# The second half of the tokens reads x by features, without transposes on TensorE

## The chip, the cores and the metric

The kernel runs on one core of a Trainium2 chip. The metric is the device time of one execution in microseconds, as the median of several runs. The engines are TensorE (PE for its matmuls, PEld for its weight loads), VectorE (DVE), ScalarE (ACT), GpSimd (POOL) and SyncE (SP), which issues most DMAs. Each works through a queue of its own in order; a semaphore wait at its head stops all that is behind it.

## The reference, cut to what matters

One residual block over 1024 tokens of 1024 features, all float32. The first lines are those of the change:

```python
def rms_norm(x, w):
    return x * rsqrt(mean(x * x, axis=-1) + 1e-6) * w

h = rms_norm(x, norm1_w) * (1 + scale1) + shift1      # shift1 .. gate2 from silu(c) @ w_ada + b_ada
x = x + gate1 * (concat[A(h), B(h)] @ w_out)          # A: gated delta rule, 4 heads x 128; B: short convolution
h = rms_norm(x, norm2_w) * (1 + scale2) + shift2
x = x + gate2 * ((silu(h @ w_gate) * (h @ w_up)) @ w_down)
return rms_norm(x, norm_f_w)
```
A and B begin with one projection `h @ w_in`. A's q, k and v go through a causal convolution over four tokens and SiLU, and then through the delta rule, which walks over the tokens in chunks of 64, so that its second half follows its first.

## The kernel before

**The projection.** Features lie on the partitions. `H[k][hf]` holds block k (128 of 1024 features) of h for one half of the tokens (`hf`, 512 tokens), as a high part, rounded for the fast matmul, and a low part, the rest; each product is three 128x512 matmuls (high by high, high by low, low by high). One column tile (128 columns of w_in by one half) is 24 of them into one PSUM bank, `acc` in the trace. `loader` fetches a tile's weights in two units (`raw`), `split_unit` splits each into high (ACT or DVE) and low (DVE), `u` in the trace, and `fill` multiplies. A task such as `q20` names tiles that need the first half alone, `z12` both halves.

**The first half.** x by tokens is normalised and transposed block by block (`xh0`), while the weights of six column tiles come in by DMA (`load0`) and `acc0` multiplies (`acc` from `whl`). Their evacuation is `first_evac`: a copy from PSUM into one of two buffers `pr`, four taps of the convolution on DVE (`cv`), SiLU on ACT.

**The second half.** `h1_load` fetches the four x tiles of tokens 512 to 1023 when the loads of the first half are issued. `norm_rs` squares and sums a tile on ACT (`jk`), adds EPS and takes the power -1/2 on POOL (`st`, `rs`). DVE scales the tile, in place. Then for each feature block `h1_work` transposes four 128x128 pieces on TensorE into a bank (`tr`), and `h_make` evacuates it: high part on ACT, the whole again as `hf` on ACT or DVE, low part on DVE (`h <- hf,h`). Two tasks `h1_work` share the eight blocks.

**What follows.** When all eight blocks stand, `ab_phase(1)` multiplies h by the columns of a and b (`ab`, 16 matmuls), the pool of the x tiles closes and the delta rule `gdn` of the first half may begin (`gT`, `gbc`, `kT`, ... and the chain of `K`, `A`, `O` with the state S), with the column tiles of the projection between its matmuls.

**What sets the order.** Up to the `o` tiles nothing of this order is written by hand. Each part is a task that asks for its next operation; a planner inside the kernel (`Sim`) holds a cost for each operation and emits, engine by engine, the one that can begin first. Within a small tolerance the smaller priority number goes first: `PR` gives `evac` 1.5, `h1` 1.8, `split` 3, `fill` 9. So one number can move every engine's queue. Buffers that the planner hands out it knows; the x tiles (`xp`, eight buffers) are handed out by the pool, and a load into a used buffer gets a semaphore wait of which the planner has no count. The MLP behind the `o` tiles is in an order written by hand.

Of the kernel before, what the change touches and what calls it, by code (L numbers as in the profile page):

```python
# [9 lines left out]
F32 = mybir.dt.float32  # L10
F32R = mybir.dt.float32r
BF16 = mybir.dt.bfloat16
AF = mybir.ActivationFunctionType
ALU = mybir.AluOpType
# [3 lines left out]
P = 128  # L18
# [3 lines left out]
KB = 8  # L22
NT = 8
HT = 512
# [13 lines left out]
HOLD = dict(pe=0.0, dve=0.12, act=0.12, sp=0.0, pool=0.0)  # L38
MARGIN = dict(pe=0.6)
BIAS = dict(dve=0.3)  # L40
PR = dict(sums0=0.35, x0=0.1, ada0=0.2, h0=0.3, w0=0.4, acc=0.5, load0=0.0, setup=0.2, hurry=0.5, chain=0, m=1, evac=1.5, a=2, v=2.5, ab=1.2, out=4, h1=1.8, split=3, y0=5, wu=5.5, x2=6, ada=7, fill=9)
TASKS = "z00 q20 s00 q30 z12 z32 z22 s32 q01 q11 z01 q21 q31 s22 s10 s11 s01".split()
CHUNKS = [(0, 4), (4, 4), (8, 3)]
STEPS = (("X", "A11", "B11", True), ("Y", "A12", "B21", True), ("X", "S2", "T2", False), ("Z", "S1", "T1", True),
# [7 lines left out]
def kernel(  # L52
    ctx: ExitStack,
    tc: tile.TileContext,
    x: bass.AP,
    c_cols: bass.AP,
    cols: bass.AP,
    w_ada: bass.AP,
# [16 lines left out]
    chain, mover = [None], [None]  # L75

    class Ordered:
# [18 lines left out]
    PE, DVE, ACT, POOL, SP = (Ordered(n, e) for n, e in (  # L96
        ("pe", nc.tensor), ("dve", nc.vector), ("act", nc.scalar), ("pool", nc.gpsimd), ("sp", nc.sync)))
# [7 lines left out]
    def nm(s):  # L105
        n_id[0] += 1
        return f"{s}_{n_id[0]}"
# [23 lines left out]
    def flat(ap):  # L131
        return ap.rearrange("p a b -> p (a b)")
# [13 lines left out]
    ident = cst.tile([P, P], F32, name="ident", tag="ident")  # L146
    make_identity(nc, ident)
    ones_r = cst.tile([P, P], F32R, name="ones", tag="ones")
    ones = ones_r.bitcast(F32)
# [11 lines left out]
    def rsqrt_pow(dst, src, n):  # L161
        return POOL.tensor_tensor(dst, src, nhalf[:, 0:n], ALU.pow)
# [7 lines left out]
    def raw_t(shape=(P, HT), dtype=F32):  # L170
        return cyclic("raw", RAW, shape, dtype)
# [10 lines left out]
    sp = s_ctx.__enter__()  # L182
    x_ctx = tc.tile_pool(name="xp", bufs=1, side="left", reuse_waits="tile")
    xp = x_ctx.__enter__()
# [3 lines left out]
    def dma(out, in_):  # L188
        SP.dma_start(out=out, in_=in_)
# [5 lines left out]
    def load_x(tt, pool, tag, bufs):  # L195
        t = pool.tile([P, D], F32, name=nm("x"), tag=tag, bufs=bufs)
        dma(t, xs[tt * P:(tt + 1) * P, :])
        return t
# [3 lines left out]
    def h_slot(k, hf):  # L202
        return hp_.tile([P, 2, HT], F32R, name=nm(f"h{k}_{hf}"), tag=f"H{k}_{hf}")
# [23 lines left out]
    x0 = [xp.tile([P, D], F32, name=nm("x"), tag="x", bufs=8) for _ in range(4)]  # L227
# [13 lines left out]
    for i in range(2):  # L241
        dg = raw_t([P, 4, P])
# [6 lines left out]
    s1c = cst.tile([P, KB], F32, name="s1c", tag="s1c")  # L249
    b1c = cst.tile([P, KB], F32, name="b1c", tag="b1c")  # L250
    nb1 = sp.tile([P, KB], F32, name="nb1", tag="nb1")
    mods = sp.tile([P, 2 * KB], F32, name="mods", tag="mods")

    def norm_rs(t, pool, tag, jt="junk"):
        junk = pool.tile([P, D], BF16, name=nm("jk"), tag=jt, bufs=1)
        st = pool.tile([P, 2], F32, name=nm("st"), tag=tag, bufs=4)
        sq = ACT.activation(junk, t, AF.Square, scale=1.0 / 32.0, accum_out=st[:, 0:1])
        p0 = POOL.tensor_scalar(st[:, 1:2], st[:, 0:1], EPS, None, ALU.add)
        rs = pool.tile([P, 1], F32, name=nm("rs"), tag=tag + "r", bufs=4)
        p1 = rsqrt_pow(rs, st[:, 1:2], 1)  # L260
        return rs, sq, p0, p1

    def xnorm(t, pool):
        rs = norm_rs(t, pool, "n1")[0]
        DVE.tensor_scalar(t, t, rs, None, ALU.mult)

    heads01 = [m0 + hd for hd in (0, 1) for m0 in (MT_K, MT_Q, MT_V)]
    late = []
    for i, t in enumerate(x0):
        rs, sq, p0, p1 = norm_rs(t, sp, "n1")  # L270
# [33 lines left out]
    class Sim:  # L304
# [18 lines left out]
        def free(self, t):  # L323
            res, i = self.owner.pop(t.tensor.name)
            res.slots.append((max([a[4] for a in self.acc.get(t.tensor.name, [])] + [0.0]), i))
            res.slots.sort()
# [228 lines left out]
    hfs, was, wrs, whls = sim.res("hf", 2), sim.res("wa", 5), sim.res("wr", 3), sim.res("whl", 2)  # L555
    raws, hls = sim.res("raw", RAW), sim.res("hl", 4)
    prs, cvs, vts, qks = sim.res("pr", 2), sim.res("cv", 2), sim.res("vT", 4), sim.res("qkT", 4)
    dense, chb = sim.res("b", 3), sim.res("b", 5, (6, 7, 3, 4, 5))
# [6 lines left out]
    def bank(res, name):  # L565
        return res.tile(psp, [P, HT], F32, name)
# [7 lines left out]
    free = sim.free  # L574
# [12 lines left out]
    def mm(out_, lhsT, rhs, start=True, stop=True):  # L587
        PE.matmul(out_, lhsT, rhs, start=start, stop=stop)

    def tr(out_, in_):  # L590
        PE.transpose(out_, in_, ident)
# [49 lines left out]
    def h_make(k, h, ps, first=None):  # L641
        hf = hfs.tile(sp, [P, HT], F32, "hf")
        ACT.activation(h[:, 0, :], ps, AF.Identity, bias=b1c[:, k:k + 1], scale=s1c[:, k:k + 1])
        if first is not None:
            first[k] = h
        if first and k:
            ACT.activation(hf, ps, AF.Identity, bias=b1c[:, k:k + 1], scale=s1c[:, k:k + 1])
        else:
            sim.either([("act", "activation", nc.scalar.activation, (hf, ps, AF.Identity), dict(bias=b1c[:, k:k + 1], scale=s1c[:, k:k + 1])),
                        ("dve", "tensor_scalar", nc.vector.tensor_scalar, (hf, ps, s1c[:, k:k + 1], b1c[:, k:k + 1], ALU.mult, ALU.add), {})])  # L650
        free(ps)
        DVE.tensor_tensor(h[:, 1, :], hf, h[:, 0, :].bitcast(F32), ALU.subtract)
        free(hf)
# [140 lines left out]
        free(scr)  # L794
        sc_[hf] = dict(beta=beta, G=G, nG=nG, eG=eG, kd=kd)

    x1 = []

    def h1_load():
        sim.wait(lambda: "loads0" in done)  # L800
        for tt in range(4, 8):
            x1.append(load_x(tt, xp, "x", 8))
        for t in x1:
            xnorm(t, sp)
        done.add("x1")

    h1_left = list(range(KB))
# [1 line left out]
    def h1_work():  # L809
        sim.wait(lambda: "x1" in done)  # L810
        while h1_left:
            k = h1_left.pop(0)
            ps = bank(chb, "tr")
            for i in range(4):
                tr(ps[:, i * P:(i + 1) * P], x1[i][:, k * P:(k + 1) * P])
            h = h_slot(k, 1)
            h_make(k, h, ps)
            H[k][1] = h
            if all(H[j][1] is not None for j in range(KB)):
                done.add("h1")  # L820
# [76 lines left out]
    def loader():  # L897
        sim.wait(lambda: "loads0" in done)
        while todo:
            sim.wait(lambda: any(may(kd_, hv_) for kd_, _, hv_ in todo))  # L900
            kind, i, halves = todo.pop(next(n for n, (kd_, _, hv_) in enumerate(todo) if may(kd_, hv_)))
            for c0, hs, evac, start in tiles_of(kind, i, halves):
# [4 lines left out]
                for n in range(2):  # L907
# [3 lines left out]
                    dma(flat(r), w_in[(c0 if c0 < AB_COL else c0 - 8) // P, :, n * HT:(n + 1) * HT])  # L911
                    sim.spawn(split_unit, lambda: PR["hurry"] if ready_u[0] < 2 else PR["split"], it, n, r)
        done.add("loaded")
# [10 lines left out]
    def fill():  # L924
        while True:
# [4 lines left out]
            for hf in it["halves"]:  # L930
                ps = bank(dense, "acc")
                for k in range(KB):
# [270 lines left out]
    def gdn(hf):  # L1203
# [252 lines left out]
    x2 = []  # L1456
# [10 lines left out]
    for _ in range(2):  # L1467
        sim.spawn(h1_work, PR["h1"])
# [253 lines left out]
    c = {p: {} for p in range(NP)}  # L1722
# [316 lines left out]
    def prod_d(ci, s, i):  # L2039
        b, an, bn, first = STEPSD[s]  # L2040
        nf = CHUNKS[ci][1]
        sets = ((2, 3, 6, 7), (4, 5, 0, 1))
        if first:
            bd_[b, i] = bank_tile(sets[(ci + (b != "X")) % 2][i], "dn")
        ps = bd_[b, i]
        sl = slice(i * P, (i + 1) * P)
        for j in range(nf):
            a, u = dm[ci, an][j], dm[ci, bn][j]
            for m, (ai, ui) in enumerate(((0, 0), (0, 1), (1, 0))):
                pmm(ps, a[ai][:, sl], u[ui], first and j == 0 and m == 0, j == nf - 1 and m == 2, not first)  # L2050
        return ps
# [55 lines left out]
    for k, (n, i) in enumerate(slots):  # L2107
        ci, s = seq_d[n]
        ps = prod_d(ci, s, i)
# [24 lines left out]
def _laid_out(a):  # L2134
    import numpy as np

    col = lambda v: v.reshape(-1, P).T
    w, wi = a["w_ada"][0], a["w_in"][0]
    d = {n: a[n] for n in ("x", "w_ada", "b_ada", "A_log", "dt_bias", "w_out", "w_gate", "w_up", "w_down", "norm_f_w")}
    d["c_cols"] = col(a["c"])  # L2140
    d["cols"] = np.concatenate([col(a[n]) for n in ("norm1_w", "b_ada", "norm2_w", "gdn_norm_w", "conv_qkv_w", "conv_short_w")], axis=1)
    d["w_mod"] = w[:, 0:2 * D].T.reshape(2, KB, P, D).transpose(1, 2, 0, 3)
    d["w_in0"] = wi[:, 0:1536].reshape(KB, P, 3, 512)[:, :, :, 0:256].reshape(KB, P, 768)
    main = np.concatenate([wi[:, 0:AB_COL], wi[:, SCB_COL:]], axis=1)
    d["w_in"] = main.reshape(KB, P, -1, P).transpose(2, 1, 0, 3).reshape(-1, P, D)
    d["w_ab"] = wi[:, AB_COL:SCB_COL].reshape(KB, P, 8).transpose(1, 0, 2).reshape(P, 64)
    d["consts"] = _constants()
    return d


_ARGS = ["x", "c_cols", "cols", "w_ada", "w_mod", "b_ada", "w_in0", "w_in", "w_ab", "A_log", "dt_bias", "w_out",
         "w_gate", "w_up", "w_down", "norm_f_w", "consts"]


# [34 lines left out]
```

## Time and profile before

| | |
|---|---|
| median of 3 runs | 1169.83 us (1169.58 to 1169.99) |
| profiled execution | 1169.63 us, of which the span of the trace is 1167.8 us |
| busy: PE, PEld, DVE, ACT, POOL | 1157.2, 968.1, 920.7, 546.1, 59.6 us |
| DMA | 207.06 MB, 177 GB/s on the mean |
| granted TensorE clock | 0.999 |

In the profile "line engine operation out<-in" names a group of instructions by the tiles that it writes and reads, without their numbers; `L450` and `L88` are helpers through which all instructions pass, so tiles and not lines tell them apart. Before, `L450` is the planned part and `L88`, `L89` the parts in a fixed order. A row of a timeline has the start, the length of a merged group and its count; a float32 matmul on plain float32 counts as two records, a transpose as one. In a list of waits the columns are total, times and longest. An order (below) lists what stands in an engine's queue, not when it runs.

### The profile page before, as it was taken

The page shows a single profiled execution, that of the slowest core. Times are in us where ns is not written, and L with a number is a line of the kernel's source. Part 1 is how long each engine was busy: PE and PEld are TensorE (multiplying, and loading weights), DVE is VectorE, ACT ScalarE, POOL GpSimd, SP SyncE. Part 2 cuts the span into 40 slices and gives each one's busy share as a digit, 9 for nine tenths or more (in the row PEclk, how much of TensorE's full clock was granted, in tenths as well). Part 3 has the DMA queues.
Part 4 walks back from the last instruction along what each step waited for, and adds up shares of the span by engine and source line. Part 5 has one row for each costly group of instructions (what it writes and reads, how often), then busy time and mean ns, then how long its engine had stood idle before and what let it go on. Part 6 is the DMA issues. An engine that isn't in the chain of part 4 may idle for free.

```text
span 1167.8 us, 16456 instructions
## 1 busy us (share of the span) xinstructions
PE 1157.2 (99%) x5582; PEld 968.1 (83%) x5582; DVE 920.7 (79%) x1702; ACT 546.1 (47%) x1182; POOL 59.6 (5%) x100
## 2 busy tenths in 40 slices
PE   9999999999999999999999999999999999999997
PEld 7888888888888888888888888888888888888886
DVE  7898988898987898669776777776777687788676
ACT  6779733458634552325433333333333365443343
POOL 1110101001101010200000000000000000000002
PEclk9999999999999999999999999999999999999999
DMA  9633455534325555434264456446554589869413
GB/s 363 246 99 110 118 171 163 168 114 137 113 66 163 163 193 175 174 101 144 80 216 158 140 201 223 159 132 222 191 184 137 194 306 393 308 203 340 144 37 145
DMA packets 126453, 207.06 MB, mean 177 GB/s; under 512 B 20513, under 2 KB 45089, under 8 KB 126369
## 3 DMA queue, kind: packets, MB, share of 16 engines
q1 hardware_dynamic: 121520, 202.86, 51.5%
q10 hardware_dynamic: 4848, 3.15, 0.9%
q8 instruction: 44, 0.72, 0.3%
q14 instruction: 41, 0.33, 0.1%
HBM read 150.91 MB, written 55.05 MB: 176 GB/s over the span
## 4 chain that ended last, share of the span: by engine, by line
PE 93%; DVE 3%; ACT 2%; DMA 1%; issue 1%; SPq 0%; ACTq 0%; DVEq 0%
PE acc L88 35%; PE acc L450 24%; PE dn L88 17%; PE o L88 4%; PE o L450 4%; PE A L450 1%; PE K L450 1%; DMA wr<-in_w_in_dram 1%; DVE xo L89 1%; PE ab L450 1%; PE w L450 1%; PE u L450 1%; PE O L450 1%; PE tr L450 1%; PE kk L450 1%
## 5 line engine op out<-in xcount | busy, mean ns | idle before, releaser
L450 PE MATMUL acc<-h,u 128*128 128x512 f32 x1200 | 301.0, 398 | 0.0
L450 PEld LDWEIGHTS acc<-h,u 128*128 128x128 f32 x1200 | 219.0, 188 | 41.1
L88 PE MATMUL acc<-h,hl 128*128 128x512 f32 x600 | 140.1, 390 | 0.0
L88 PEld LDWEIGHTS acc<-h,hl 128*128 128x128 f32 x600 | 112.4, 188 | 23.2
L88 PE MATMUL acc<-h,u 128*128 128x512 f32 x456 | 106.1, 389 | 0.0
L88 PE MATMUL acc<-T,hl 128*128 128x512 f32 x432 | 101.4, 390 | 0.4 <-ACT cc L89 0.4
L88 PEld LDWEIGHTS acc<-h,u 128*128 128x128 f32 x456 | 85.6, 188 | 17.7
L88 PEld LDWEIGHTS acc<-T,hl 128*128 128x128 f32 x432 | 80.9, 188 | 17.5 <-ACT cc L89 0.9
L88 PE MATMUL dn<-h,h 128*128 128x512 f32 x396 | 90.7, 389 | 0.0
L89 DVE TENSOR_TENSOR xo<-xo,dn 128x512 f32<-128x512 f32 x84 | 57.0, 683 | 42.3 <-PE dn L88 34.8
L89 ACT COPY cc<-acc 128x512 f32<-128x512 f32 x66 | 38.4, 590 | 108.3 <-PE acc L88 108.3
L88 PEld LDWEIGHTS dn<-h,h 128*128 128x128 f32 x396 | 74.3, 188 | 15.4
L88 PE MATMUL acc<-T,u 128*128 128x512 f32 x360 | 84.0, 389 | 0.0
L88 PEld LDWEIGHTS acc<-T,u 128*128 128x128 f32 x360 | 67.6, 188 | 14.0
L450 ACT CAST u<-raw 128x512 fp32r<-128x512 f32 x69 | 42.7, 622 | 66.0 <-PE acc L450 64.3
L89 DVE TENSOR_TENSOR cc<-cc,acc 128x512 f32<-128x512 f32 x66 | 43.8, 682 | 29.8 <-PE acc L88 29.8
L89 DVE TENSOR_TENSOR hl<-R,hl 128x512 fp32r<-128x512 f32 x60 | 39.4, 687 | 33.5 <-ACT hl L89 33.4
L450 DVE TENSOR_TENSOR u<-raw,u 128x512 fp32r<-128x512 f32 x82 | 56.0, 685 | 11.9 <-ACT u L450 11.7
L450 DVE SCALAR_TENSOR_TENSOR cv<-pr,cols_a,cv 128x512 f32<-128x512 f32 x72 | 52.9, 745 | 0.1
L89 ACT CAST h<-rw 128x512 fp32r<-128x512 f32 x57 | 32.7, 618 | 40.5 <-PE dn L88 34.6
L89 ACT CAST hl<-R 128x512 fp32r<-128x512 f32 x60 | 35.7, 622 | 23.5 <-DVE R L89 10.7
L89 DVE TENSOR_TENSOR u<-R,u 128x512 fp32r<-128x512 f32 x46 | 30.1, 686 | 20.6 <-ACT u L89 20.5
(343 smaller groups left out, 1993.2 us busy)
## 6 DMA issues: line engine op xcount, KB each, us to landing
raw<-in_w_in_dram SPq DMA_DIRECT2D x82, 256.0 KB, 3.1
am_scr<-cc SPq DMA_DIRECT2D x77, 256.0 KB, 4.6
raw<-in_w_ada_dram SPq DMA_DIRECT2D x56, 256.0 KB, 3.4
rw<-am_scr SPq DMA_DIRECT2D x55, 256.0 KB, 5.2
rw<-bm_scr SPq DMA_DIRECT2D x53, 256.0 KB, 5.3
bm_scr<-raw SPq DMA_DIRECT2D x51, 256.0 KB, 5.4
R<-in_w_gate_dram SPq DMA_DIRECT2D x22, 512.0 KB, 4.3
R<-in_w_up_dram SPq DMA_DIRECT2D x22, 512.0 KB, 5.5
```

Of the source, the lines that this page charges most:

```text
L88: return call(*a, **k)
L89: ins = call(*a, **k)
L450: ins = call(*a, **k)
```

## The change

The host lays out a second copy of the second half's x, by features (`x_t`, eight blocks of 128 features by 512 tokens). `h1_load` fetches four tiles of two blocks each (`xt`). The x by tokens is still fetched and squared, for the norm alone: `norm_rs` writes the four factors into the columns of `rs1`; a diagonal of them is multiplied by ones on TensorE, one plain float32 matmul 128x512, which puts the factor of token c into column c of all partitions (`RS`). For each block DVE makes `hf` = xt * scale column * RS, ACT adds the bias into the high part, and DVE makes the low part from `hf`, bias and high part. The scaling of x on DVE, the 32 transposes and the evacuations of their banks go. `h1` gets priority 1.3 instead of 1.8, ahead of `evac`.

```diff
-PR = dict(... evac=1.5, a=2, v=2.5, ab=1.2, out=4, h1=1.8, split=3, ...)
+PR = dict(... evac=1.5, a=2, v=2.5, ab=1.2, out=4, h1=1.3, split=3, ...)
...
-    def norm_rs(t, pool, tag, jt="junk"):
+    def norm_rs(t, pool, tag, jt="junk", rs=None):
...
-        rs = pool.tile([P, 1], F32, name=nm("rs"), tag=tag + "r", bufs=4)
+        if rs is None:
+            rs = pool.tile([P, 1], F32, name=nm("rs"), tag=tag + "r", bufs=4)
...
-    x1 = []
+    x1t, rs1 = [], sp.tile([P, 4], F32, name="rs1", tag="rs1")
+    RS = sp.tile([P, HT], F32, name="RS", tag="RS")
 
     def h1_load():
         sim.wait(lambda: "loads0" in done)
-        for tt in range(4, 8):
-            x1.append(load_x(tt, xp, "x", 8))
-        for t in x1:
-            xnorm(t, sp)
+        for j in range(4):
+            t = xp.tile([P, 2, HT], F32, name=nm("xt"), tag="x", bufs=8)
+            dma(t, x_t[2 * j:2 * j + 2].rearrange("k p c -> p k c"))
+            x1t.append(t)
+        for i in range(4):
+            t = load_x(4 + i, xp, "x", 8)
+            norm_rs(t, sp, "n1", rs=rs1[:, i:i + 1])
+        dg = raw((P, 4, P))
+        DVE.tensor_tensor(dg, bc1(ident, 4), bc2(rs1, P), ALU.mult)
+        ps = bank(chb, "RS")
+        mm(ps, ones, flat(dg))
+        free(dg)
+        ecopy(RS, ps)
+        free(ps)
         done.add("x1")
...
             k = h1_left.pop(0)
-            ps = bank(chb, "tr")
-            for i in range(4):
-                tr(ps[:, i * P:(i + 1) * P], x1[i][:, k * P:(k + 1) * P])
             h = h_slot(k, 1)
-            h_make(k, h, ps)
+            hf = hfs.tile(sp, [P, HT], F32, "hf")
+            DVE.scalar_tensor_tensor(hf, x1t[k // 2][:, k % 2], s1c[:, k:k + 1], RS, ALU.mult, ALU.mult)
+            ACT.activation(h[:, 0, :], hf, AF.Identity, bias=b1c[:, k:k + 1])
+            DVE.scalar_tensor_tensor(h[:, 1, :], hf, b1c[:, k:k + 1], h[:, 0, :].bitcast(F32), ALU.add, ALU.subtract)
+            free(hf)
             H[k][1] = h
...
+    d["x_t"] = a["x"][0, HT:].T.reshape(KB, P, HT)
```

Three places of the new order. TensorE first, in the column tiles after `ab` of the first half. Before, transposes of a block stand between the matmuls of a tile:

```order
L450 MATMUL acc_771<-h_0_86_518,u_695 128x512 x2
L450 MATMUL tr_821<-ident,x_405 128x128
L450 MATMUL tr_821<-ident,x_428 128x128
L450 MATMUL tr_821<-ident,x_436 128x128
L450 MATMUL tr_821<-ident,x_441 128x128
L450 MATMUL acc_771<-h_0_86_518,u_695 128x512
```
The change has one row in their place, 26 matmuls behind `ab` of the first half:

```order
L448 MATMUL acc_559<-h_0_86_519,u_464 128x512 x3
L448 MATMUL acc_707<-h_0_37_240,u_565 128x512 x2
L448 MATMUL RS_698<-raw_677,ones 128x512
L448 MATMUL acc_707<-h_0_37_240,u_565 128x512
L448 MATMUL acc_707<-h_0_44_274,u_565 128x512 x3
```
After RS 70 matmuls follow (the rest of three tiles), and then the 16 of `ab` of the second half, the last two of them on the last block; before, these stand behind the last transposes, later by 35 matmuls. From the products `P` of the second half's delta rule on, both orders are the same on TensorE.

DVE, at the end of the work on the second half's h. Before, the low parts stand singly among taps of the convolution (`cv`) and low parts of weights (`u`):

```order
L450 TENSOR_TENSOR h_1_135_757<-hf_758,h_1_135_757 128x512
L450 TENSOR_TENSOR u_795<-raw_773,u_795 128x512
L450 SCALAR_TENSOR_TENSOR cv_814<-pr_790,cols_a,cv_814 128x512
L450 MEMSET pr_831 128x3
L450 SCALAR_TENSOR_TENSOR cv_814<-pr_790,cols_a,cv_814 128x512
L450 COPY halo<-pr_831 128x3
L450 TENSOR_SCALAR cv_852<-pr_831,cols_a 128x512
L450 SCALAR_TENSOR_TENSOR cv_814<-pr_790,cols_a,cv_814 128x512
L450 TENSOR_TENSOR u_829<-raw_801,u_829 128x512
L450 SCALAR_TENSOR_TENSOR cv_852<-pr_831,cols_a,cv_852 128x512
L450 TENSOR_TENSOR h_1_148_826<-hf_827,h_1_148_826 128x512
```
In the change (`hf` from `xt`, then the low part of h) the taps of the two first-half tiles `cv_730` and `cv_757` are left until the last blocks are done:

```order
L448 TENSOR_TENSOR u_823<-raw_804,u_823 128x512
L448 TENSOR_SCALAR raw_694<-raw_694 128x16
L448 SCALAR_TENSOR_TENSOR hf_842<-xt_443,s1c,RS 128x512
L448 SCALAR_TENSOR_TENSOR h_1_155_835<-hf_836,b1c,h_1_155_835 128x512
L448 SCALAR_TENSOR_TENSOR cv_730<-pr_689,cols_a,cv_730 128x512
L448 SCALAR_TENSOR_TENSOR h_1_157_841<-hf_842,b1c,h_1_157_841 128x512
L448 SCALAR_TENSOR_TENSOR cv_730<-pr_689,cols_a,cv_730 128x512
L448 SCALAR_TENSOR_TENSOR cv_757<-pr_732,cols_a,cv_757 128x512
L448 TENSOR_TENSOR u_850<-raw_828,u_850 128x512
L448 SCALAR_TENSOR_TENSOR cv_757<-pr_732,cols_a,cv_757 128x512
```
Their buffers `pr` come free only behind them, and the next column tiles are copied out of PSUM into those buffers.

SP's queue, behind the small loads of `setup`. Before, four x tiles and then the weights of the first column tiles:

```order
L450 DMA raw_420<-in_w_ab_dram 128x64
L450 DMA x_405<-in_x_dram 128x1024
L450 DMA x_428<-in_x_dram 128x1024
L450 DMA x_436<-in_x_dram 128x1024
L450 DMA x_441<-in_x_dram 128x1024
L450 DMA raw_406<-in_w_in_dram 128x512
L450 DMA raw_452<-in_w_in_dram 128x512
```
In the change the tiles by features come first, and the x by tokens, the first of which goes into a buffer of the first half's x, stand among the weights:

```order
L448 DMA raw_422<-in_w_ab_dram 128x64
L448 DMA xt_407<-in_x_t_dram 128x2x512
L448 DMA xt_430<-in_x_t_dram 128x2x512
L448 DMA xt_438<-in_x_t_dram 128x2x512
L448 DMA xt_443<-in_x_t_dram 128x2x512
L448 DMA x_448<-in_x_dram 128x1024
L448 DMA raw_408<-in_w_in_dram 128x512
L448 DMA raw_459<-in_w_in_dram 128x512
L448 DMA raw_563<-in_w_in_dram 128x512
L448 DMA x_575<-in_x_dram 128x1024
```

More of the change, by code (lines that the diff above doesn't have):

```diff
@@ L40 @@
 BIAS = dict(dve=0.3)
-PR = dict(sums0=0.35, x0=0.1, ada0=0.2, h0=0.3, w0=0.4, acc=0.5, load0=0.0, setup=0.2, hurry=0.5, chain=0, m=1, evac=1.5, a=2, v=2.5, ab=1.2, out=4, h1=1.8, split=3, y0=5, wu=5.5, x2=6, ada=7, fill=9)
+PR = dict(sums0=0.35, x0=0.1, ada0=0.2, h0=0.3, w0=0.4, acc=0.5, load0=0.0, setup=0.2, hurry=0.5, chain=0, m=1, evac=1.5, a=2, v=2.5, ab=1.2, out=4, h1=1.3, split=3, y0=5, wu=5.5, x2=6, ada=7, fill=9)
 TASKS = "z00 q20 s00 q30 z12 z32 z22 s32 q01 q11 z01 q21 q31 s22 s10 s11 s01".split()
@@ L55 @@
     x: bass.AP,
+    x_t: bass.AP,
     c_cols: bass.AP,
@@ L258, in norm_rs @@
         p0 = POOL.tensor_scalar(st[:, 1:2], st[:, 0:1], EPS, None, ALU.add)
-        rs = pool.tile([P, 1], F32, name=nm("rs"), tag=tag + "r", bufs=4)
+        if rs is None:
+            rs = pool.tile([P, 1], F32, name=nm("rs"), tag=tag + "r", bufs=4)
         p1 = rsqrt_pow(rs, st[:, 1:2], 1)
         return rs, sq, p0, p1
-    def xnorm(t, pool):
-        rs = norm_rs(t, pool, "n1")[0]
-        DVE.tensor_scalar(t, t, rs, None, ALU.mult)
     heads01 = [m0 + hd for hd in (0, 1) for m0 in (MT_K, MT_Q, MT_V)]
@@ L2148, in _laid_out @@
     return d
-_ARGS = ["x", "c_cols", "cols", "w_ada", "w_mod", "b_ada", "w_in0", "w_in", "w_ab", "A_log", "dt_bias", "w_out",
+_ARGS = ["x", "x_t", "c_cols", "cols", "w_ada", "w_mod", "b_ada", "w_in0", "w_in", "w_ab", "A_log", "dt_bias", "w_out",
          "w_gate", "w_up", "w_down", "norm_f_w", "consts"]
```

## The prediction

> **What bounds the kernel now.** I read the page first, then TensorE's waits, its busy time by stretch, and the timeline of the stretch that the change touches.
>
> ```profile
> span 1167.8 us, 16456 instructions
> PE 1157.2 (99%) x5582; PEld 968.1 (83%) x5582; DVE 920.7 (79%) x1702; ACT 546.1 (47%) x1182; POOL 59.6 (5%) x100
> PE 93%; DVE 3%; ACT 2%; DMA 1%; issue 1%; SPq 0%; ACTq 0%; DVEq 0%
> ```
> The last line is the chain that ended last by engine. 93% of it is TensorE. The waits of TensorE's matmuls over the whole span (in total, times, longest), and three stretches (length, busy time of PE, PEld, DVE, ACT, POOL, then clock, DMA share, GB/s), say the same:
>
> ```profile
> PE heat L88 <- POOL nhalf L89: 1.4, 1, 1.4
> PE acc L450 <- ACT h L450: 1.1, 1, 1.1
> PE acc L88 <- ACT cc L89: 0.4, 1, 0.4
> PE y L450 <- DVE pr L450: 0.4, 1, 0.4
> PE A L450 <- DVE S L450: 0.2, 1, 0.2
> PE ps L88 <- DVE raw L89: 0.2, 1, 0.2
> ```
>
> ```profile
> 16.00:52.00 36.00, 36.00 (x170) 29.26 (x169) 31.74 (x59) 26.42 (x47) 2.37 (x5) 1.00 0.90 348
> 52.00:90.00 38.00, 38.00 (x187) 31.43 (x186) 36.25 (x76) 28.88 (x49) 5.37 (x6) 1.00 0.25 80
> 1150.00:1168.00 18.00, 11.12 (x49) 8.85 (x48) 11.08 (x19) 7.00 (x18) 3.73 (x7) 0.93 0.47 174
> ```
> All waits come to 3.7 us, and 6.9 lie behind the last matmul (18.00 - 11.12); with the busy 1157.2 that is the whole span. So an instruction taken out of its queue is worth what it holds there, as long as nothing new makes it wait. The second stretch is that of the change: DVE is busy 36.25 of 38 us in it, and that is where a new wait could come from.
>
> A busy share alone would not prove this. The Trainium skill says so (Perfetto Trace Analysis, Identifying the Most-Contended Engine): matmul occupancy is a poor measure for TensorE, and weight loads tell more. Here those are at 83%, so by that page alone the transposes might lie in slack, and the sum would be near zero. What decides is the start-to-start spacing below.
>
> **Transposes removed.** A stretch of TensorE's timeline (start, length of the merged group, instruction, count):
>
> ```profile
> 66.57 6.64 PE L450 MATMUL acc<-h,u 128*128 128x512 f32 x28
> 73.05 0.60 PE L450 MATMUL tr<-ident,x 128*128 128x128 f32 x4
> 73.40 4.83 PE L450 MATMUL acc<-h,u 128*128 128x512 f32 x20
> ...
> 85.72 1.18 PE L450 MATMUL acc<-h,u 128*128 128x512 f32 x4
> 86.74 0.60 PE L450 MATMUL tr<-ident,x 128*128 128x128 f32 x4
> ```
> From a group of four transposes to the next matmul are 73.40 - 73.05 = 0.35 us. Eight such groups are 2.8 us. There is a second cost, at the edges. 28 matmuls take 73.05 - 66.57 = 6.48 us, 4 take 86.74 - 85.72 = 1.02: 24 more cost 5.46, or 0.2275 each, so the run of four pays 0.11 beyond 4 x 0.2275. Each interruption of the 128x512 stream costs about that; eight go, 0.9 us. Together -3.7 us.
>
> The duration column reads otherwise:
>
> ```profile
> L450 PE MATMUL tr<-ident,x x64: 270/272/273, 8.8 to 87.1; 128*128 128x128 f32 x64
> ```
> 272 ns is what one transpose shows, though the starts are 0.09 us apart. The Trainium skill (TensorE: Matmul & The Clock Gate, Part 4: PE-mode transpose) gives about 275 ns for one inside a kernel. The trace agrees on that as a latency. Taken as a price, 32 of them are 8.8 us instead of 3.7, and the time would be about 1161.5 us (an estimate from that page). The spacing of starts decides against it.
>
> **One matmul added: RS.** It is 128x512 on plain float32, a kind that runs before only at the very start (two in the first two rows below). Its warm neighbour is a group of four 128x128 float32 products, also 512 columns:
>
> ```profile
> 3.70 2.61 PE L88 MATMUL ps<-raw,ones 128*128 128x512 f32 x4 [0.18 <-DVE raw L89]
> 6.14 2.84 PE L88 MATMUL heat<-ident,ones 128*128 128x128 f32 x24
> ...
> 109.49 1.05 PE L450 MATMUL kk<-qkT 128*128 128x128 f32 x8
> 110.30 0.48 PE L450 MATMUL acc<-h,u 128*128 128x512 f32 x1
> ```
> Ends: 0.81 us (110.30 - 109.49) and 1.22 us ((6.14 - 3.70) / 2, waits included). I take 0.81, the warm one, plus one interruption: +0.9 us.
>
> **Order on TensorE elsewhere.** The other matmuls are the same ones, planned into another order up to about 260 us. Counted in the two orders, the 128x512 stream is broken 11 times less often; eight minus one are explained above, four are chance merges of small groups: -0.4 us. Sum on TensorE: -3.7 + 0.9 - 0.4 = -3.2 us.
>
> **DVE and ACT.** Prices and places, single rows out of the timelines of DVE, ACT, POOL and PE (STT is the scalar_tensor_tensor):
>
> ```profile
> 50.50 0.75 DVE L450 TENSOR_SCALAR x<-x,rs 128x1024 f32<-128x1024 f32 x1
> 51.16 4.06 DVE L450 SCALAR_TENSOR_TENSOR cv<-pr,cols_a,cv 128x512 f32<-128x512 f32 x6
> 67.56 0.81 DVE L450 TENSOR_SCALAR hf<-tr,s1c,b1c 128x512 f32<-128x512 f32 x1 [0.28 <-ACT h L450]
> 89.34 0.69 DVE L450 TENSOR_TENSOR h<-hf,h 128x512 fp32r<-128x512 f32 x1 [0.38 <-ACT hf L450]
> 86.00 0.78 ACT L450 ACTIVATE h<-tr,b1c,s1c 128x512 fp32r<-128x512 f32 x1
> 47.10 1.65 ACT L450 CAST u<-raw 128x512 fp32r<-128x512 f32 x3
> 55.75 0.59 ACT L450 COPY raw<-ab 128x512 f32<-128x512 f32 x1 [0.49 <-PE ab L450]
> 57.90 1.04 ACT L450 ACTIVATE jk<-x 128x1024 bf16<-128x1024 f32 x1
> 59.84 1.02 POOL L450 TENSOR_TENSOR rs<-st,nhalf 128x1 f32<-128x1 f32 x1
> 51.88 3.83 PE L450 MATMUL ab<-h,wab 128*128 128x512 f32 x16
> 55.55 2.21 PE L450 MATMUL acc<-h,u 128*128 128x512 f32 x9
> ```
> DVE loses four scalings of x (3.0 us), one hf (0.8) and eight subtractions (5.5), and gains 16 STT at 4.06 / 6 = 0.68 (10.8) and the diagonal for RS (0.7): +2.2 us net. ACT drops 15 passes over PSUM at 0.78 and gains eight from SBUF (0.55, as the casts) and one copy (0.59): about -6.7 us. Neither sets the end by itself, so I cost both at nothing, if TensorE stays covered. The cover: RS stands 26 matmuls and a group of transposes after 55.55, at about 62.0 us, and ends at 62.9; its copy on ACT (0.6) lets DVE begin at 63.5. From there to the last h DVE has 18 STT (16 for h, two of the conv), five lo parts of weights at 0.69 and small ones: 12.2 + 3.6, so the last h stands at about 79.3 us (in before, 89.34 + 0.69 = 90.0). TensorE reaches `ab` of this half 70 matmuls after RS, at 78.9 us, but needs the last h only with the last of its 16, at 82.4. Margin 3 us. One wait is new: RS waits for the diagonal, that for the fourth x's norm on POOL, and every matmul behind RS stands with it. In the new order the fourth square follows ACT's copy of `ab` directly, at 56.3; from a square's begin to POOL's end are 59.84 + 1.02 - 57.90 = 3.0 us, the diagonal takes 0.7, so RS could run from about 60.0 and stands at 62.0. Margin 2 us.
>
> **DMA.** 2 MB more are read, and the new x tiles lie in the buffers of the first half's x, whose last transposes run at 40.44:
>
> ```profile
> 35.27 3.91 SPq L450 DMA_DIRECT2D x<-in_x_dram x4
> 39.76 20.27 SPq L450 DMA_DIRECT2D raw<-in_w_in_dram x8
> ...
> 40.44 0.60 PE L450 MATMUL tr<-ident,x 128*128 128x128 f32 x4
> ```
> SP's queue stands at the first x until about 41.0, so the w_in loads behind it issue some 2 us later, with 0.5 MB (1.5 us at 348 GB/s) ahead of them. They are cast from 47.1 on and multiplied from 55.55 on: 3.5 us late at most, hidden by some 5 us. If the cover were gone, they would cost those 3.5.
>
> **Waits that stay.** The first chain of the delta rule and the output after it lose a little in before: 0.2 us at `A`, 0.4 at `y`, in the list of waits above. The order there is new, so these may vanish (-0.6) or grow. In the new order the second `A` of the chain has three matmuls less between `K` and itself (3 x 0.2275 = 0.7 us of cover for DVE's update of S). I take no change for the likeliest, and -0.6 to +0.8 as its range.
>
> **Rivals.** (1) New waits eat the gain: in the chain between DVE's S and TensorE's A, or at RS. For it speaks DVE at 95% and the changed order; against it, the 2 to 3 us margins. One to four microseconds lost: about 1168.5 us, no measurable change. (2) Slower: the evacuations of the first half's tiles now rank below h on DVE. TensorE's fifth tile, behind `ab` at 82.6, needs a bank that ACT's copy into `pr` empties; one of the two `pr` must come free first, and the last STT that reads it stands right behind the last h: 80.0, copied by 80.6. A margin of 2.0 us. For it speaks that everything on DVE in this stretch hangs on one engine 95% busy; against it, that the same queue kept TensorE fed in before. Every microsecond of DVE beyond the margin stops TensorE for one; from 5.2 us of lateness on the kernel is slower, and by over 0.2% from 7.5 us, say 1174 us. (3) Transposes count in full: 1161.5. (4) They lay in slack and nothing is gained: 1169.6.
>
> **How the numbers follow.** The profiled execution took 1169.63 us, 0.20 under the median of 1169.83. 1169.63 - 3.2 = 1166.4; with 0.2 for the unevenness of the waits' range and for RS, whose other end is 0.4 dearer, I say 1166.6. What a measurement tells from no change is 0.2%, 2.34 us. Chances: the forecast 0.64 (1165.6 to 1167.4), rival 1 0.19, rival 2 0.12, rival 3 0.02, rival 4 0.03. Faster 0.66, within 0.2% 0.22, slower 0.12. The range leaves out rivals 2 and 3 and the far part of 1: 1165.2 to 1169.2.
>
> **What would show it.** Right: no `tr<-ident,x` between 52 and 90 us, RS at about 62 us with some 0.8 us to the next matmul, `ab` of the second half near 79 instead of 89.50, TensorE's total wait still near 3.7 us, and the whole later timeline earlier by about 3 us. Wrong: a wait of TensorE on RS's diagonal, on DVE's h, on a PSUM copy, or on S in the chain, longer than 0.7 us together.

## The result and the profile after

The changed kernel took 1166.07 us (median of 7 runs, 1165.08 to 1166.65), the one before, beside it, 1169.99 us (median of 7, 1169.30 to 1171.41). The ratio is 0.9963 with a 95% interval of 0.9954 to 0.9973: faster by 0.37%, or 4.3 us of 1170 (3.2 to 5.4). The profiled execution of the changed kernel took 1166.65 us, the longest of its seven, with a span of 1164.9 us.

The page of the changed kernel (span; busy time and instructions of each engine; the chain that ended last, by engine):

```profile
span 1164.9 us, 16388 instructions
PE 1154.4 (99%) x5552; PEld 965.7 (83%) x5552; DVE 921.1 (79%) x1702; ACT 542.7 (47%) x1181; POOL 61.9 (5%) x100
PE 94%; DVE 2%; DMA 2%; ACT 1%; issue 1%; SPq 0%; ACTq 0%; DVEq 0%
```

What TensorE's matmuls waited for in it (in total, times, longest):

```profile
PE heat L89 <- POOL ident masks.py:199: 1.4, 1, 1.4
PE acc L448 <- ACT h L448: 1.1, 1, 1.1
PE A L448 <- DVE S L448: 0.4, 1, 0.4
PE ada L448 <- DVE qs L448: 0.4, 1, 0.4
```

The stretch of the change in it (length; busy time of PE, PEld, DVE, ACT, POOL; clock, DMA share, GB/s):

```profile
52.00:90.00 38.00, 38.00 (x173) 31.16 (x172) 36.39 (x87) 31.46 (x57) 6.52 (x8) 1.00 0.26 86
```

TensorE's busy time fell by 2.8 us (from 1157.2) and its listed waits from 3.7 to 3.3 us. It still has no pause in the stretch of the change. DVE stays as full as it was, 36.39 of 38 us. ACT is busier in this stretch (31.46 after 28.88) and less busy in all (542.7 after 546.1).

Rows of TensorE's timeline of the changed kernel, out of four places:

```profile
52.22 3.79 PE L448 MATMUL ab<-h,wab 128*128 128x512 f32 x16
...
58.25 4.12 PE L448 MATMUL acc<-h,u 128*128 128x512 f32 x17
62.20 1.02 PE L448 MATMUL RS<-raw,ones 128*128 128x512 f32 x2
62.66 16.47 PE L448 MATMUL acc<-h,u 128*128 128x512 f32 x70
78.97 3.79 PE L448 MATMUL ab<-h,wab 128*128 128x512 f32 x16
...
91.28 0.27 PE L448 MATMUL gT<-ident,ghl 128*128 128x128 f32 x1
...
326.80 0.60 PE L448 MATMUL qT<-ident,qkT 128*128 128x128 f32 x4
327.15 18.19 PE L448 MATMUL acc<-h,u 128*128 128x512 f32 x79
```

The last two answer to these of the kernel before, at the end of the part whose order the change touches:

```profile
330.12 0.60 PE L450 MATMUL qT<-ident,qkT 128*128 128x128 f32 x4
330.48 17.73 PE L450 MATMUL acc<-h,u 128*128 128x512 f32 x77
```

The transposes between 52 and 90 us are gone, the stream of 128x512 matmuls runs 70 long behind RS, and `ab` of the second half stands at 78.97 instead of 89.50. From `ab` of the first half to the long run behind the last `qT`, TensorE took 330.48 - 51.88 = 278.60 us before and takes 327.15 - 52.22 = 274.93 us now: 3.67 us less. The two profiled executions differ by 0.34 us ahead of this, to the changed kernel's loss, and by 0.43 us behind it, so the spans differ by 2.9 us. The medians differ by 3.9, and by the ratio it is 4.3; no trace shows where the last microsecond lies.

### The profile page after: what moved, and what is told of

Read it like the earlier page. It is cut to its first block, busy times and chain, and to the rows that moved or that the text cites. A ratio compares the mean times of both kernels' runs of the same rounds, so it can differ in the third digit from the quotient of the medians.

```text
span 1164.9 us, 16388 instructions
## 1 busy us (share of the span) xinstructions
PE 1154.4 (99%) x5552; PEld 965.7 (83%) x5552; DVE 921.1 (79%) x1702; ACT 542.7 (47%) x1181; POOL 61.9 (5%) x100
## 4 chain that ended last, share of the span: by engine, by line
PE 94%; DVE 2%; DMA 2%; ACT 1%; issue 1%; SPq 0%; ACTq 0%; DVEq 0%
PE acc L89 35%; PE acc L448 25%; PE dn L89 17%; PE o L89 4%; PE o L448 4%; PE A L448 1%; PE K L448 1%; DMA wr<-in_w_in_dram 1%; DVE xo L90 1%; PE ab L448 1%; PE kk L448 1%; PE O L448 1%; PE u L448 1%; PE w L448 1%; DVE T L90 1%
## 5 line engine op out<-in xcount | busy, mean ns | idle before, releaser
L448 PE MATMUL acc<-h,u 128*128 128x512 f32 x1200 | 298.4, 397 | 0.0
L448 PEld LDWEIGHTS acc<-h,u 128*128 128x128 f32 x1200 | 219.4, 188 | 42.2 <-issue 0.5
L448 ACT CAST u<-raw 128x512 fp32r<-128x512 f32 x66 | 40.7, 621 | 63.7 <-PE acc L448 60.3
L448 DVE TENSOR_TENSOR u<-raw,u 128x512 fp32r<-128x512 f32 x82 | 56.1, 686 | 9.1 <-ACT u L448 8.9
L448 DVE SCALAR_TENSOR_TENSOR cv<-pr,cols_a,cv 128x512 f32<-128x512 f32 x72 | 53.4, 748 | 0.9 <-ACT cv L448 0.5
```

The source lines that it names most:

```text
L448: ins = call(*a, **k)
```

## The experiments

Each result is given as a ratio to the kernel before, run beside it on the same chip. "Against the changed kernel" is (ratio - 0.9963) x 1170 us; each of the two ratios has an interval of about 1.1 us to either side.

| run | median us (runs) | ratio to before (95%) | against the changed kernel |
|---|---|---|---|
| tr_back | 1169.65 (11) | 0.9990 (0.9981 to 0.9999) | +3.2 |
| rs_8more | 1173.15 (10) | 1.0022 (1.0013 to 1.0031) | +6.9 |
| rs_quarters | 1173.08 (10) | 1.0024 (1.0015 to 1.0034) | +7.1 |
| dve_2more | 1166.84 (7) | 0.9972 (0.9961 to 0.9982) | +1.1 |
| dve_8more | 1172.21 (11) | 1.0015 (1.0006 to 1.0024) | +6.1 |
| xt_twice | 1180.05 (4) | 1.0083 (1.0070 to 1.0097) | +14.0 |
| xt_copy | 1169.60 (11) | 0.9998 (0.9989 to 1.0007) | +4.1 |
| h1_18 | 1173.90 (5) | 1.0035 (1.0022 to 1.0047) | +8.4 |
| h1_11 | 1168.69 (11) | 0.9985 (0.9976 to 0.9994) | +2.6 |
| h1_03 | 1176.70 (5) | 1.0055 (1.0042 to 1.0068) | +10.8 |
| before_h1_13 | 1172.10 (11) | 1.0014 (1.0005 to 1.0023) | (kernel before, +1.6 on itself) |

My theory was that of the prediction: TensorE is the bound, so the transposes taken out are the gain, RS costs its own time, and everything else is covered. The rivals were that the gain comes from the new order, that DVE sets the end of this stage, and that the added traffic eats a part.

### The transposes alone: tr_back

The 32 transposes stand in TensorE's queue again, four ahead of each block's h, now of the x tiles by tokens as they were fetched (`x1`, unscaled), into a bank that nobody reads. All the other queues keep their order.

```diff
+            ps = bank(chb, "tr")
+            for i in range(4):
+                seq("pe", nc.tensor.transpose(ps[:, i * P:(i + 1) * P], x1[i][:, k * P:(k + 1) * P], ident))
+            free(ps)
             h = h_slot(k, 1)
```


> The changed kernel with the 32 transposes of the second half's x put back on TensorE, into a bank that nobody reads, at the places where the eight blocks are made (seven groups, since two blocks begin together); every other queue has the order of the changed kernel. Theory (a transpose is worth the spacing of starts, 0.089 us, and a group 0.11 us for the interruption): 2.84 + 7 x 0.11 = 3.6 us more than the changed kernel, so about 1169.7 us, level with the kernel before. Rival (a transpose is worth its duration of 0.272 us): 8.7 us more, 1174.8. Rival (transposes lie in slack, the gain came from the new order): no change, 1166.

Its TensorE timeline:

```profile
68.22 0.60 PE L825 MATMUL tr<-ident,x 128*128 128x128 f32 x4
68.57 0.95 PE L448 MATMUL acc<-h,u 128*128 128x512 f32 x3
...
95.12 0.27 PE L448 MATMUL gT<-ident,ghl 128*128 128x128 f32 x1
```
`gT` comes 95.12 - 91.28 = 3.84 us later, and 3.95 when the 0.11 us by which this execution reached `ab` sooner (52.11) are added. The median is 3.2 us above the changed kernel by the ratios. That is near what the spacing of starts had said (3.6 for the seven groups here, 3.7 for the eight before), and far from 32 x 272 ns = 8.7 us or from nothing. On this point the Trainium skill (TensorE: Matmul & The Clock Gate, Part 4: PE-mode transpose) names about 275 ns for a bf16 transpose of 128x128 inside a kernel. As the length of one, that agrees with the 272 ns of the float32 ones here; as the price of one in a full queue it doesn't, which is 3.95 / 32 = 0.12 us here.

### RS alone: rs_8more and rs_quarters

RS is multiplied eight more times, into the same bank and with the same result: once as the kernel does it, and once as four matmuls of 128 columns each.

```diff
         mm(ps, ones, flat(dg))
+        for _ in range(8):
+            seq("pe", nc.tensor.matmul(ps, ones, flat(dg), start=True, stop=True))
```
```diff
         mm(ps, ones, flat(dg))
+        for _ in range(8):
+            for i in range(4):
+                seq("pe", nc.tensor.matmul(ps[:, i * P:(i + 1) * P], ones, dg[:, i], start=True, stop=True))
```


> The changed kernel with the RS matmul issued eight times more, the same product into the same bank. If a plain float32 128x512 matmul costs 0.81 us, as the prediction had it from four 128-column ones, the kernel takes 6.5 us more, 1172.6; if it costs 0.46, the spacing seen after RS in the changed kernel, 3.7 us more, 1169.8. The later RS also moves h back by as much, which the second half's margin (the last h stands 2.4 us before its matmul) does not feel, since TensorE is moved back with it.

> The changed kernel with eight more RS products, each as four matmuls of 128 columns in place of one of 512, none of them read. The prediction took its price for RS from four products of 128 columns (0.81 us). Eight of 512 columns cost 6.86 us. If a plain float32 product costs by its columns alone, the 32 here take 6.5 to 7.0 us (1172.6 to 1173.1); if each matmul has a fixed part of its own that shows at 128 columns, 8 us and over (1174 and over).

TensorE's timeline of the first:

```profile
63.05 7.03 PE L812 MATMUL RS<-raw,ones 128*128 128x512 f32 x16
69.52 16.47 PE L448 MATMUL acc<-h,u 128*128 128x512 f32 x70
...
98.14 0.27 PE L448 MATMUL gT<-ident,ghl 128*128 128x128 f32 x1
```
`gT` is 98.14 - 91.28 = 6.86 us later, with `ab` of the first half at the same 52.22: 0.86 us for each of eight. In the other run `ab` began 0.59 us sooner and `gT` stood at 97.83, so eight cost 97.83 - 91.28 + 0.59 = 7.14 us, 0.89 each. In these two runs the columns are what is paid, not the matmul. The prediction's 0.81, from four products of 128 columns, was the right neighbour. In the changed kernel's own timeline the run behind RS starts 0.46 us after RS; whoever took that for the price would have been wrong by half. The rest shows behind it: the first three matmuls after RS take 1.26 us, three after a group of transposes 0.95 (the row at 68.57 above). The Trainium skill (FP8 and Floating Point Precision, TensorE Precision Notes) says that true FP32 takes four passes through the array. With the 0.2275 us of one 128x512 matmul in the prediction for a pass, an estimate from that page is 0.91 us; the 0.86 to 0.89 measured come near it.

### DVE: dve_2more and dve_8more

The first STT of the second half's operand is done two or eight times more, writing the same values.

```diff
+            for _ in range(8 if k == 0 else 0):
+                seq("dve", nc.vector.scalar_tensor_tensor(hf, x1t[0][:, 0], s1c[:, 0:1], RS, ALU.mult, ALU.mult))
             DVE.scalar_tensor_tensor(hf, x1t[k // 2][:, k % 2], s1c[:, k:k + 1], RS, ALU.mult, ALU.mult)
```


> The changed kernel, with two more of the first scalar-tensor-tensor on VectorE (hf from xt, s1c and RS, 0.68 us each), which write the same values again; every other queue keeps its order. The stages after it come up to 1.36 us later on VectorE, and TensorE's order is unchanged. Theory (VectorE is covered, by margins of 0.8 to 1.4 us: gT waits for a row ready at 90.41 and starts at 91.28, the fifth tile's bank is free at 81.24 and its tile starts at 82.60): the time goes up by 0 to 0.6 us, 1166.1 to 1166.7. Rival 'VectorE's burst already sets the end of this stage': the whole 1.36 us appears, 1167.5. Rival 'covered by several us, as the 79% of VectorE suggests': 0, 1166.1.

> The same with eight more, 5.4 us of VectorE. Theory: the margin of 0.8 to 1.4 us is used up, and the rest appears as waits of TensorE between the second half's ab and gbc: +4.0 to +4.6 us, 1170.1 to 1170.7, so that the change would be worth nothing with a VectorE slower by this. 'Already the bound': +5.4, 1171.5. 'Covered by several us': under 1 us, below 1167.1.

TensorE's timeline with eight more (in brackets the idle time ahead, and what ended it):

```profile
73.01 8.00 PE L448 MATMUL acc<-h,u 128*128 128x512 f32 x34 [1.45 <-DVE pr L448]
...
84.00 0.50 PE L448 MATMUL ab<-h,wab 128*128 128x512 f32 x1 [0.27 <-ACT h L448]
84.97 0.74 PE L448 MATMUL ab<-h,wab 128*128 128x512 f32 x2 [0.47 <-DVE h L448]
86.30 0.51 PE L448 MATMUL ab<-h,wab 128*128 128x512 f32 x1 [0.59 <-DVE h L448]
87.58 2.11 PE L448 MATMUL acc<-h,u 128*128 128x512 f32 x8 [0.77 <-ACT pr L448]
...
96.85 0.30 PE L448 MATMUL gT<-ident,ghl 128*128 128x128 f32 x1 [0.15 <-DVE raw L448]
```
`gT` is 96.85 - 91.28 - 0.14 = 5.43 us later (0.14 is the later start, `ab` at 52.36), the time is 6.1 us longer, and the change is worth nothing any more. With two more `gT` stands at 92.28, 0.72 us later when the start (`ab` at 52.50) is taken off; the time is 1.1 us longer, an amount that the intervals don't tell from 0 or 1.4. I had expected 4.0 to 4.6 us and 0 to 0.6.

It looks as if the margins that I had read weren't there. DVE's rows say otherwise. `gT` reads `ghl`, the last row of each block below (the list above names `raw`, DVE's next row, which ends some 0.1 us later); the changed kernel, two more, and eight more:

```profile
90.24 0.17 DVE L448 TENSOR_TENSOR ghl<-G,ghl 128x16 fp32r<-128x16 f32 x1
```
```profile
64.16 1.54 DVE L825 SCALAR_TENSOR_TENSOR hf<-xt,s1c,RS 128x512 f32<-128x512 f32 x2 [1.30 <-ACT RS L448]
...
91.96 0.17 DVE L448 TENSOR_TENSOR ghl<-G,ghl 128x16 fp32r<-128x16 f32 x1
```
```profile
64.02 6.26 DVE L825 SCALAR_TENSOR_TENSOR hf<-xt,s1c,RS 128x512 f32<-128x512 f32 x8 [1.30 <-ACT RS L448]
...
72.27 0.69 DVE L448 TENSOR_TENSOR u<-raw,u 128x512 fp32r<-128x512 f32 x1
...
96.53 0.17 DVE L448 TENSOR_TENSOR ghl<-G,ghl 128x16 fp32r<-128x16 f32 x1
```
At `ghl` DVE is late by 91.96 - 90.24 - 0.28 = 1.44 us with two more, and by 96.53 - 90.24 - 0.14 = 6.15 with eight, not by 1.36 and 5.4. The added STT are dearer than 0.68 us each (the next row on DVE starts at 70.21, so eight take 6.19 us). They also stand ahead of a tap and two small rows that in the changed kernel run while DVE waits for RS, so DVE waits 1.30 us there instead of 0.51; most of that is made up later. TensorE lost 0.72 of the 1.44 us and 5.43 of the 6.15: a cover of 0.72 us in both runs. That is the margin at the row itself: in the changed kernel `ghl` ends at 90.41 and `gT` starts at 91.28, 0.87 us later, and in both runs with added work `gT` starts 0.15 us after the end of `ghl`. So the margin was there, and the lateness was taken too small.

The other margins held too. With two more, TensorE is late by 0.12 us at the fifth tile (83.00 for 82.60, less 0.28), whose bank had a margin of 1.4, and by the whole 0.72 only at `gT`. With eight more it stops first at 73.01, in the middle of a column tile: the 37th matmul behind RS is the first to read the low part of that tile's second unit of weights, the `u` that DVE ends at 72.27 + 0.69 = 72.96. (The list names `pr`, a small row of DVE that ends 0.01 us later.) The rival that DVE already sets the pace is nearer than the one with several us of cover, but 0.7 us were left.

### The added traffic: xt_twice and xt_copy

First each of the four transfers of `xt` was issued twice, then each was followed by a copy of the same 0.5 MB into an unused area of DRAM.

```diff
+            seq("sp", nc.sync.dma_start(out=t, in_=x_t[2 * j:2 * j + 2].rearrange("k p c -> p k c")))
             dma(t, x_t[2 * j:2 * j + 2].rearrange("k p c -> p k c"))
```
```diff
             dma(t, x_t[2 * j:2 * j + 2].rearrange("k p c -> p k c"))
+            seq("sp", nc.sync.dma_start(out=x_cp[2 * j:2 * j + 2], in_=x_t[2 * j:2 * j + 2]))
```


> The changed kernel with each of the four transfers of x by features issued twice (2.1 MB more; the second copy of a pair writes the same bytes). x by tokens, of which the norms are made, and the next columns of w_in come later by the 4 to 6 us that 2.1 MB take at the 394 GB/s of this stretch. Theory: the 2.1 MB that the change adds were hidden with 2 to 5 us to spare, and this takes more than is to spare: RS, which the order puts at 62.2, has its diagonal ready at 60.5, so TensorE waits 2.5 to 5 us there or at the tile whose w_in is late: +2 to +5 us, 1168 to 1171. Rival 'the traffic is hidden by far': under 0.5 us, 1166.6 or less. Rival 'the traffic was never hidden': all of it, +5.3 us and over, and then half of the change's gain had been lost to it.

The first missed by far, because it isn't what I took it for: the second transfer into a tile waits on SP until the first has landed, so SP stood four times. `xt_twice`, SP's queue, ScalarE, TensorE and stretches of TensorE:

```profile
41.05 1.13 SPq L803 DMA_DIRECT2D xt<-in_x_t_dram  x1
46.49 0.37 SPq L448 DMA_DIRECT2D xt<-in_x_t_dram  x1
...
56.88 0.42 SPq L448 DMA_DIRECT2D x<-in_x_dram  x1
```
```profile
61.29 1.06 ACT L448 ACTIVATE jk<-x 128x1024 bf16<-128x1024 f32 x1 [14.95 <-DMA x<-in_x_dram]
...
62.34 0.57 ACT L448 COPY pr<-acc 128x512 f32<-128x512 f32 x1
```
```profile
62.96 4.21 PE L448 MATMUL acc<-h,u 128*128 128x512 f32 x9 [7.19 <-ACT pr L448]
69.81 1.12 PE L448 MATMUL abt<-ident,raw 128*128 128x128 f32 x4 [2.64 <-ACT raw L448]
70.58 6.29 PE L448 MATMUL acc<-h,u 128*128 128x512 f32 x17
```
```profile
56.00:63.00 7.00, 0.04 (x1) 0.04 (x1) 0.99 (x3) 1.71 (x4) 0.48 (x1) 0.65 0.76 284
63.00:70.00 7.00, 4.36 (x10) 2.97 (x11) 6.90 (x17) 6.58 (x13) 3.50 (x6) 0.50 0.81 315
70.00:80.00 10.00, 10.00 (x34) 7.85 (x34) 8.41 (x21) 6.51 (x12) 1.52 (x3) 0.74 0.23 75
```
It shows where lateness of x goes, though: into ScalarE. The square of x stands in ScalarE's queue ahead of the copies that empty TensorE's banks, so they wait for x too. TensorE waited 7.19 + 2.64 = 9.83 us, and then ran at a granted clock of 0.50 and 0.74: its 17 matmuls took 6.29 us instead of 4.12.

> The changed kernel, with each of the four transfers of x by features followed on the queue by a copy of the same 0.5 MB into an area of DRAM that nobody reads: 2.1 MB more for the DMA engines, and no transfer that waits for another to land, as in the run with the transfers issued twice. What follows on the queue comes later by about 5.3 us (2.1 MB at the 394 GB/s of this stretch). There, ScalarE's first square came 13.96 us late and TensorE waited 9.83 us, so the theory puts the cover at 4.1 us: +5.3 us leave 1.2 us of waits, and with the lower clock behind a wait 1 to 3 us, 1167.1 to 1169.1. Rival 'no cover, ScalarE's wait for x is passed on whole': +5 us or more, 1171 and over. Rival 'the traffic is hidden by far': under 0.5 us, 1166.6 or less.

The second is the experiment that I had meant. Its profile:

```profile
59.73 0.66 PE L449 MATMUL abt<-ident,raw 128*128 128x128 f32 x4 [1.38 <-ACT raw L449]
...
64.10 1.02 PE L449 MATMUL RS<-raw,ones 128*128 128x512 f32 x2
```
```profile
51.22 1.06 ACT L449 ACTIVATE jk<-x 128x1024 bf16<-128x1024 f32 x1 [4.34 <-DMA x<-in_x_dram]
```
ScalarE's first square began 51.22 - 47.33 = 3.89 us later than in the changed kernel (its row there: `47.33 1.06 ACT L448 ACTIVATE jk<-x`), of which 0.30 is a later start of the whole (`ab` at 52.52). Of the 3.59 left, TensorE lost 1.60 (RS at 64.10 instead of 62.20, less 0.30), and as much still at `gT`, 93.18. So the cover is 2.0 us of lateness of x, not 4.1, and the change's own traffic lies within it, since TensorE doesn't wait there. The profiled execution, 1168.34 us, is the shortest of eleven, which reach to 1172.81; by the ratio the kernel lost 4.1 us, more than the 1 to 3 us expected. What the longer ones lost beside those 1.6 us no trace shows.

### The rank: h1_18, h1_11, h1_03 and before_h1_13

The changed kernel with the second half's operand at rank 1.8, the rank of before (h1_18; the diff), and likewise at 1.1 (h1_11) and 0.3 (h1_03); and the kernel before with the rank of the changed one (the second diff).

```diff
-PR = dict(... h1=1.3, ...)
+PR = dict(... h1=1.8, ...)
```
```diff
-PR = dict(... h1=1.8, ...)
+PR = dict(... h1=1.3, ...)
```


> The changed kernel with the priority of h1 back at 1.8, so that the first half's evacuations rank ahead again. Theory (the gain is TensorE's own time, the order costs or gives little): within 1 us of the changed kernel, 1165 to 1167. Rival (the new rank gave the gain): back to about 1169 to 1170.

> The kernel before with the priority of h1 at 1.3 and nothing else. Theory: the rank alone gains nothing, 1169 to 1171. Rival (the rank is half of the gain): about 1168 or less.

> The changed kernel with the second half's operand ranked over the first half's ab as well (1.1 for 1.3). TensorE's order up to the second half's ab is the same, behind it G stands ahead of abt. Theory (the rank matters because the second half's gates must be out of the way before the planned part runs out of work; once they are, a higher rank can add nothing): 1166.1, plus or minus 1 us, which is what two orders of the same work have differed by. Rival 'the earlier the better': 1 to 3 us less, 1163 to 1165. Rival 'the first half starves': 2 us or more above, 1168 and over.

> The changed kernel with the second half's operand ranked first of all but the loads (0.3 for 1.3); the second half's ab stands three rows of TensorE earlier, G and abt later behind it. If the time falls steadily with the rank (1.8: +8 us, 1.3: 0), it is 1165 or less; if ranks above the column tiles are only other orders of the same work (1.1: +2.6 us), it is 1166 to 1170, and no lower than the changed kernel by more than 1 us.

With 1.8 the changed kernel is slower than the one before, 8.4 us above the changed one, where I had thought the rank worth little. `ab` of the second half falls to 99.31 us there (before: 89.50), the last `O` of the second half's chain to 444.0 (429.4 in the changed kernel), and at the end of the planned part TensorE runs out of other work. That run's TensorE timeline, and the ten microseconds behind it:

```profile
478.15 0.40 PE L89 MATMUL o<-wu,kt 128*128 128x512 f32 x1
480.56 0.49 PE L89 MATMUL row<-Tt,ones 128*128 128x512 f32 x1 [2.00 <-ACT Tt L448]
```
```profile
480.00:490.00 10.00, 9.07 (x31) 6.75 (x31) 5.49 (x6) 4.67 (x9) 3.12 (x8) 0.83 0.82 327
```
Two further waits, 1.5 us of `K` for DVE's `A` and 0.9 us of `tr` for DVE's x, stand in the same list. How the 8.4 us divide among these, the lower clock and order I haven't measured.

The rank alone, without the other changes, costs the kernel before 1.6 us. So the new rank isn't the gain by itself, and without it the gain of the transposes turns into a loss. Nor is earlier better: 1.1 costs 2.6 us (TensorE's listed waits are 4.1 us there for 3.3, so most of it is open), 0.3 costs 10.8. In the last, the second half's gates come among the heads of the first half, and TensorE waits for ScalarE:

```profile
123.57 1.11 PE L448 MATMUL kT<-ident,qkT 128*128 128x128 f32 x4 [4.87 <-ACT qkT L448]
128.15 1.22 PE L448 MATMUL acc<-h,u 128*128 128x512 f32 x2 [3.46 <-ACT pr L448]
```
The granted clock was 0.51 in the stretch from 123 to 130 us of that run. Of the four ranks run, 1.3 is the fastest. No version here beats the changed kernel.

## Why the prediction was right, and where it was not

The prediction said 1166.6 us (1165.2 to 1169.2) and faster. The ratio's 4.3 us (3.2 to 5.4) are somewhat more than its sum of 3.2. Step by step:

- **TensorE is the bound.** Right: in three runs work was put into its queue alone, and what it made `gT` later came out at the end, within the intervals (3.95 us at `gT` and 3.2 at the end; 6.86 and 6.9; 7.14 and 7.1).
- **Transposes, -3.7.** Right, measured as 3.95 at `gT`. The rival that took the 272 ns of the duration column as the price (1161.5), and the one with the transposes in slack (1169.6), fall.
- **RS, +0.9.** Right: 0.86 to 0.89 each. The sign that was to show it, some 0.8 us from RS to the next matmul, didn't come: 0.46, with the rest in the matmuls behind.
- **Order elsewhere, -0.4.** Right in size as far as it can be seen: the stretch from `ab` to the last `qT` lost 3.67, of which -3.95 + 0.87 = -3.08 are transposes and RS, so -0.6 is left. By the medians it may be more: tr_back has the transposes and RS, and is still 1.2 us (0.1 to 2.2) faster than the kernel before, which with RS's 0.9 would leave some 2 us to the order. Its trace doesn't show this (a span of 1168.6 us for 1167.8), but it is that of the longest of its eleven executions. How much the order gives stays open. The step was luckier than it looks. I had counted breaks of the stream in the given order, which is sound, but I hadn't seen how much hangs on that order: other ranks of the same work cost 2.6 to 10.8 us.
- **DVE's cover, 2 to 3 us.** Wrong: it is 0.7 us. The two rows that the prediction priced are near what it had worked out: the last h ends 0.7 us later, the fifth tile's bank is free at 81.24 for a tile at 82.60, a margin of 1.4 for 2.0. The rows of the changed kernel are:

```profile
79.21 0.75 DVE L448 SCALAR_TENSOR_TENSOR h<-hf,b1c,h 128x512 fp32r<-128x512 f32 x1
```
```profile
80.65 0.59 ACT L448 COPY pr<-acc 128x512 f32<-128x512 f32 x1 [0.82 <-DVE cv L448]
```
  But the smallest margin stands a stage later, at `gT`, where the prediction hadn't looked. Rival 2 (slower by a late DVE) had the right mechanism, though not the row that sets the cover. It put no gain at 5.2 us of lateness (a margin of 2.0 and the 3.2 gained) and 0.2% slower at 7.5; with 6.15 us the kernel was slower than before by 0.15% (0.06 to 0.24). It didn't come about in the change, since DVE is no fuller in this stretch than before (36.39 us for 36.25).
- **DVE +2.2 us, ACT -6.7, costed at nothing.** The cost was right, the sizes weren't: +0.4 and -3.4 us over the whole kernel. On ACT, the eight high parts take 0.72 us each for the 0.55 assumed, and the new plan moves other work between the two engines, in both directions: five products `u<-vT,bv`, for one, go from DVE (6 for 11) to ACT (26 for 21).
- **RS's diagonal, margin 2 us.** Right: DVE ended it at 59.81 + 0.68 = 60.49, 1.7 us ahead of RS (62.20).
- **DMA hidden.** Right, with 2.0 us to spare before ScalarE passes the lateness on. The prediction had looked at the late columns of w_in (hidden by some 5 us), and left out the first thing to be late: the square on ScalarE, which waits for x in front of the bank copies.
- **Waits that stay, -0.6 to +0.8.** Right: `y`'s 0.4 went, `A` has 0.4 for 0.2, and an `ada` of 0.4 is new: 3.3 for 3.7 in all. Rival 1 (new waits eat the gain) didn't come about.

## What to carry to other kernels

Where one engine is full, price what is taken out of its queue by the spacing of starts over a long stretch, with the interruption of the stream, and neither by the duration column nor by a single next start. The cover of an engine is the smallest margin of all the rows that it feeds, and here that one stood a stage behind the rows looked at. Work added to test a cover counts by the lateness that it makes at the row that is waited for, not by its price on paper: here 6.15 us for 5.4. A rank or a due time that comes with an edit is a part of it: here the edit without its rank, and the rank without its edit, were both slower than before, and the two together faster.

## What the runs showed of the hardware that I had not expected

- The idle times listed ahead of TensorE's matmuls are less than what those waits cost. With eight more STT they add up to 1.45 + 0.27 + 0.47 + 0.59 + 0.77 + 0.15 = 3.70 us, and `gT` came 5.43 us later, with a granted clock of 1.00 from 60 to 100 us. With two more nothing is listed, and 0.72 us are lost. In the run with the copies 1.38 us are listed and 1.60 lost. A part of it is how the trace counts: the idle time starts at the end of a record, and a record of these matmuls is 0.40 us long on the mean by the profile's page (397 ns) while the next one in a full stream starts after 0.2275. That is about 0.17 us for each wait, or 1.0 of the 1.73 us missing above; the rest is open.
- A wait of 2.00 us with a further 0.23 behind it was enough to halve the granted clock (the run at rank 1.8): it is 0.50 from 482 to 485 us and 1.00 again from 486, which is the 0.83 over ten microseconds above. 9.83 us of waits gave 0.50 to 0.74. The Trainium skill (TensorE: Matmul & The Clock Gate, Part 1) has the clock fall to half after an idle window of some 3.4 us, counted by windows that run freely. The runs with waits of several microseconds agree with the half (0.50, 0.51); in the one at 2.00 us the clock fell after a pause shorter than that window.
